# Transposes of softmax weights in longer runs on TensorE

## The chip, the cores and the metric

The kernel runs on one core of one Trainium2 chip. The metric is the device time of one execution in microseconds. The core's engines run side by side, each in the order of its own instruction stream, and wait for each other by semaphores: TensorE (PE; its weight loads are listed as PEld), VectorE (DVE), ScalarE (ACT), GpSimd (POOL) and SyncE (SP), which issues most of the transfers.

## The reference, cut to what matters

One encoder layer is applied to two sequences of 2048 tokens, each 1024 wide. Two attentions work side by side on one normed input, their outputs are gated and joined, and an output projection and a gated addition follow.

```python
proj = rms_norm(x, norm_w) @ w_in
q_a, k_a, v_a, g_a, q_b, k_b, v_b, g_b = jnp.split(proj, IN_SPLITS, axis=-1)
...
o_a = windowed_gqa_sink(q_a, k_a, v_a, sink_a) * jax.nn.silu(g_a)
...
o_b = neighbourhood_attn(q_b, k_b, v_b, rpb_b) * jax.nn.silu(g_b)
x = x + jnp.concatenate([o_a, o_b], axis=-1) @ w_out
gate = jax.nn.sigmoid(x @ w_ple_gate)
return x + (p @ w_ple) * gate
```

In the first attention (A, eight query heads on two key heads) a token sees the tokens at most 128 away, with a learned sink in the softmax. In the second (B, eight heads) the tokens form a grid of 32 rows by 64 columns, and each sees a window of 8 by 16 with a learned bias.

## The kernel before, in words

All is float32. Operands of products are split into a high and a low part; a projection takes three products for one. TensorE's work is a stream of projection products into which the attention's steps are put at chosen places.

The loop at line 1253 runs over 96 steps. Steps 0 to 31 are first attention, a block of 128 tokens each, in two halves (one for each key head): 64 units. Steps 32 to 95 are second attention, a tile of 8 by 16 tokens and four heads each: 64 units. While a unit's attention steps are issued, the stream issues the projections of a later block: each 512-wide product counts 215 and each 256-wide one 112 (lines 554, 602, 635, 883, 910). A step of first attention has 13008 of this count, its two halves half of it each; one of second attention has 10320, that is 48 products.

Where an attention step stands in the stream is written in three tables of (share of the unit, 1 for this unit or 0 for the one before, act, index): `PLAN_A` for first attention, `PLAN_C` for 51 units of second attention (`copied_`, line 112), and `PLAN_B` for its other 13. `plan` sorts the entries by share, and entries of one share keep their order. The loop lets the stream run until its count has reached an entry's share and then issues the act. TensorE's instructions keep this order exactly (`pinned`, line 272); those of the other engines are ordered by the framework's scheduler from their dependences and their place in the program, unless `P` pins them.

The acts that matter here:

- `sc`: scores of a head or pair into a PSUM tile, which VectorE adds to the mask or bias and writes to SBUF with the maximum (line 306).
- `exp`: exponentials on ScalarE (line 331). In the units of `PLAN_C`, a DMA from ScalarE's queue then copies each head's weights into a tile `tn` of another type (line 340); in first attention `turn` does it into `tna`, from SyncE's queue. Transposes of copied tiles are at line 291, of others at line 293.
- `pt`: transposes a group of the softmax weights on TensorE into a PSUM tile. In first attention there are three groups for a unit, of two, four and four transposes; in second attention one for each of the four heads, of three or four. ScalarE then copies the group as the high part (lines 813, 819, 1059) and VectorE subtracts for the low part (lines 814, 821, 1060).
- `po`: the product of transposed weights and values. `fin`: transposes the gate into PSUM, multiplies and stores.

PSUM tiles come from three sets (`PSB`, line 72). Scores, groups of transposed weights and the gate's transposes all take from the set `sc`, which has three buffers used in turn (`PSM`, line 73): a taker waits until the one three places before it has been read. For a unit of second attention the takers are four scores, the gate of the unit before and four groups, nine in all. The projections' results take from `pj`, the others from `ms`.

Of the kernel before, what the change touches and what calls it, by code (L numbers as in the profile page):

```python
# [58 lines left out]
def bias_offsets():  # L59
# [32 lines left out]
KB = 23  # L92
PLAN_A = (
    (0.04, 1, "sc", 0), (0.08, 1, "sc", 1), (0.11, 1, "sc", 2), (0.12, 1, "rest", 0), (0.14, 1, "sc", 3),
    (0.14, 1, "rest", 1), (0.21, 0, "pt", 0), (0.26, 0, "pt", 1), (0.30, 1, "qcopy", 0), (0.31, 0, "pt", 2),
    (0.32, 1, "exp", 0), (0.33, 1, "turn", 0), (0.33, 1, "turn", 1), (0.44, 1, "twice", 0),
    (0.48, 0, "po", 0), (0.56, 0, "po", 1), (0.64, 1, "prep", 0), (0.66, 0, "po", 2), (0.67, 1, "den", 0), (0.74, 0, "fin", 0),
    (0.75, 1, "gcopy", 0),
# [6 lines left out]
PLAN_C = (  # L105
    (0.00, 1, "sc", 0), (0.01, 0, "po", 0), (0.03, 1, "sc", 1), (0.05, 0, "po", 1), (0.07, 1, "sc", 2), (0.09, 0, "po", 2),
    (0.11, 1, "sc", 3), (0.16, 0, "po", 3), (0.16, 1, "exp", 0), (0.24, 0, "fin", 0), (0.35, 1, "prep", 0),
    (0.64, 1, "pt", 0), (0.73, 1, "pt", 1), (0.82, 1, "pt", 2), (0.91, 1, "pt", 3),
)


# [1500 lines left out]
```

## Time and profile before

| what | value |
|---|---|
| median of 3 runs | 2419.87 us (2417.95 to 2422.71) |
| profiled execution, its own time | 2419.81 us |
| span of the profile | 2417.8 us |
| TensorE busy | 2406.4 us (100%) |
| VectorE busy | 1733.2 us (72%) |
| ScalarE busy | 1425.4 us (59%) |
| GpSimd busy | 850.8 us (35%) |

The span runs from the first instruction to the last. A matmul is counted as busy until its modelled end, and matmuls overlap in TensorE's pipeline; so a stretch on TensorE is best read from one start to the next, not from the busy time of one instruction.

### The profile page before, as it was taken

The page shows a single profiled execution, that of the slowest core. Times are in us where ns is not written, and L with a number is a line of the kernel's source. Part 1 is how long each engine was busy: PE and PEld are TensorE (multiplying, and loading weights), DVE is VectorE, ACT ScalarE, POOL GpSimd, SP SyncE. Part 2 cuts the span into 40 slices and gives each one's busy share as a digit, 9 for nine tenths or more (in the row PEclk, how much of TensorE's full clock was granted, in tenths as well). Part 3 has the DMA queues.
Part 4 walks back from the last instruction along what each step waited for, and adds up shares of the span by engine and source line. Part 5 has one row for each costly group of instructions (what it writes and reads, how often), then busy time and mean ns, then how long its engine had stood idle before and what let it go on. Part 6 is the DMA issues. An engine that isn't in the chain of part 4 may idle for free.

```text
span 2417.8 us, 41537 instructions
## 1 busy us (share of the span) xinstructions
PE 2406.4 (100%) x12942; PEld 2031.4 (84%) x12942; DVE 1733.2 (72%) x4227; ACT 1425.4 (59%) x3408; POOL 850.8 (35%) x1373
## 2 busy tenths in 40 slices
PE   9999999999999999999999999999999999999999
PEld 7888888888888888888888888888888888888887
DVE  7888888888875776666667666776537565776876
ACT  6777777777764665666566666666753222344433
POOL 4555555556553554454445434443100000000000
PEclk9999999999999999999999999999999999999999
DMA  7665555655665677678877777778886455856765
GB/s 238 223 199 198 197 192 160 197 194 198 215 223 171 224 233 245 227 232 262 272 232 227 253 250 245 245 261 281 318 287 221 157 172 185 270 174 206 248 224 173
DMA packets 313660, 539.61 MB, mean 223 GB/s; under 512 B 36288, under 2 KB 136416, under 8 KB 309216
## 3 DMA queue, kind: packets, MB, share of 16 engines
q1 hardware_dynamic: 283776, 497.77, 61.6%
q10 hardware_dynamic: 29664, 39.19, 5.3%
q8 instruction: 104, 1.70, 0.3%
q14 instruction: 116, 0.95, 0.1%
HBM read 307.72 MB, written 134.23 MB: 183 GB/s over the span
## 4 chain that ended last, share of the span: by engine, by line
PE 95%; DMA 2%; ACT 1%; DVE 1%; issue 0%; POOL 0%; ACTq 0%; SPq 0%; DVEq 0%
PE pqk L287 14%; PE pvg L287 14%; PE acca L1402 14%; PE accc L1402 11%; PE pg L287 7%; PE pq L287 7%; PE pple L287 4%; PE scb L287 4%; PE pk L287 3%; PE pob L287 3%; PE po L287 3%; PE sc L287 3%; PE ptb L291 2%; PE pt L291 2%; PE ptb L293 1%; PE pktb L293 1%
## 5 line engine op out<-in xcount | busy, mean ns | idle before, releaser
L287 PE MATMUL pvg<-wb,xr 128*128 128x512 f32 x1536 | 472.4, 408 | 0.5 <-DMA wb<-sp_1wb 0.4
L287 PE MATMUL pqk<-wa,xr 128*128 128x512 f32 x1536 | 431.2, 408 | 0.0
L331 ACT ACTIVATE s<-s,nm 128x320 f32<-128x320 f32 (+6 forms) x512 | 294.5, 579 | 38.6 <-DVE nm L324 29.0
L287 PEld LDWEIGHTS pvg<-wb,xr 128*128 128x128 f32 x1536 | 272.8, 189 | 33.6 <-DMA wb<-sp_1wb 1.6
L287 PEld LDWEIGHTS pqk<-wa,xr 128*128 128x128 f32 x1536 | 264.9, 188 | 39.3
L1384 ACT CAST opd<-raw 128x512 fp32r<-128x512 f32 x224 | 131.5, 618 | 269.7 <-PE acca L1402 116.9
L417 POOL TENSOR_TENSOR xr<-stx,xr 128x512 fp32r<-128x512 f32 x186 | 238.0, 1296 | 102.0 <-ACT xr L416 71.6
L1385 DVE TENSOR_TENSOR opd<-raw,opd 128x512 fp32r<-128x512 f32 x224 | 146.3, 685 | 146.4 <-ACT opd L1384 146.4
L287 PE MATMUL pq<-wa,xr 128*128 128x512 f32 x768 | 240.5, 404 | 0.0
L287 PE MATMUL pg<-wb,xr 128*128 128x512 f32 x768 | 229.9, 405 | 0.7 <-DVE vv L574 0.4
L306 DVE CUSTOM_DVE_ANT_0 s<-scb,bias 128x288 f32<-128x288 f32 (+3 forms) x256 | 139.2, 547 | 71.2 <-PE scb L287 48.8
L1078 ACT COPY otb<-pob 64x512 f32<-64x512 f32 x128 | 74.3, 581 | 183.2 <-PE pob L287 182.6
L1402 PE MATMUL accc<-opd,wb 128*128 128x512 f32 x768 | 176.7, 389 | 0.0
L1402 PE MATMUL acca<-opd,wa 128*128 128x512 f32 (+1 forms) x780 | 175.9, 386 | 0.5 <-ACT raw L1487 0.5
L1402 PE MATMUL acca<-opd,s 128*128 128x512 f32 x768 | 175.4, 389 | 0.0
L1402 PEld LDWEIGHTS acca<-opd,wa 128*128 128x128 f32 x780 | 145.0, 188 | 30.2 <-ACT raw L1487 0.7
L1402 PEld LDWEIGHTS accc<-opd,wb 128*128 128x128 f32 x768 | 144.2, 188 | 29.9
L1402 PEld LDWEIGHTS acca<-opd,s 128*128 128x128 f32 x768 | 144.2, 188 | 29.9
L170 POOL TENSOR_TENSOR yb<-vrb,power 128x8 f32<-128x8 f32 x64 | 106.2, 1660 | 143.5 <-DVE vrb L898 130.9
L287 PEld LDWEIGHTS pg<-wb,xr 128*128 128x128 f32 x768 | 135.4, 188 | 17.8 <-DVE vv L574 0.8
L287 PEld LDWEIGHTS pq<-wa,xr 128*128 128x128 f32 x768 | 132.4, 188 | 11.4
L306 DVE CUSTOM_DVE_ANT_0 s<-sc,mask 128x320 f32<-128x320 f32 (+2 forms) x256 | 121.1, 478 | 19.2 <-PE sc L287 10.9
(209 smaller groups left out, 5122.4 us busy)
## 6 DMA issues: line engine op xcount, KB each, us to landing
tna<-s SPq DMA_DIRECT2D x112, 320.0 KB
stx<-x_b SPq DMA_DIRECT2D x128, 256.0 KB
vw<-v_d SPq DMA_DIRECT2D x96, 256.0 KB
v_d<-vb SPq DMA_DIRECT2D x64, 256.0 KB
xres<-x_r SPq DMA_DIRECT2D x64, 256.0 KB
raw<-x_d SPq DMA_DIRECT2D x16, 1024.0 KB
stx<-x_a SPq DMA_DIRECT2D x62, 256.0 KB
stn<-x_n SPq DMA_DIRECT2D x62, 256.0 KB
```

The costliest lines, as they stand in the source:

```text
L170: nc.gpsimd.tensor_tensor(out=y, in0=v, in1=power.broadcast_to([128, n]), op=ALU.pow)
L287: pinned(nc.tensor.matmul(out, lhsT, rhs, start=start, stop=stop))
L291: pinned(nc.tensor.transpose(out.bitcast(F32R), in_, eye))
L293: pinned(nc.tensor.transpose(out, in_, eye.bitcast(F32)))
L306: nc.vector.tensor_tensor_reduce(out=s, in0=ps[:, :n], in1=bias, scale=1.0, scalar=-3.0e38, op0=ALU.add, op1=ALU.max, accum_out=sm["mx"][: ...
L331: ex = nc.scalar.activation(ss[i], ss[i], AF.Exp, bias=nm[:, i:i + 1], accum_out=den[:, i:i + 1])
L417: low.tensor_tensor(out=lo, in0=raw, in1=hi.bitcast(F32), op=ALU.subtract)
L1078: nc.scalar.copy(ot[a:a + 64], pq[z:z + 64])
L1384: P(nc.scalar.copy(hi, v))
L1385: P(nc.vector.tensor_tensor(out=lo, in0=v, in1=hi.bitcast(F32), op=ALU.subtract))
L1402: pinned(nc.tensor.matmul(ps[:, cols], w[k][:, a, c:c + 128], o[:, b, cols], start=i in (0, 1, 4) and k == 0 and j == 0, stop=k == 3 and j ...
```

## The change

Six shares of two tables are altered; nothing else is. In first attention group 0 and group 1 get one share, so that their transposes (two and four) follow each other with no projection product between. In the 51 units of second attention that `PLAN_C` serves, the four heads' groups become two pairs, each of six to eight transposes in a row. `PLAN_B` is as before.

```diff
 PLAN_A = (
...
-    (0.14, 1, "rest", 1), (0.21, 0, "pt", 0), (0.26, 0, "pt", 1), (0.30, 1, "qcopy", 0), (0.31, 0, "pt", 2),
+    (0.14, 1, "rest", 1), (0.235, 0, "pt", 0), (0.235, 0, "pt", 1), (0.30, 1, "qcopy", 0), (0.31, 0, "pt", 2),
...
 PLAN_C = (
...
-    (0.64, 1, "pt", 0), (0.73, 1, "pt", 1), (0.82, 1, "pt", 2), (0.91, 1, "pt", 3),
+    (0.70, 1, "pt", 0), (0.70, 1, "pt", 1), (0.87, 1, "pt", 2), (0.87, 1, "pt", 3),
 )
```

## Rows read from the trace of the kernel before

**Rows 1.** The page's engine table: busy time, share of the span, instructions.

```profile
PE 2406.4 (100%) x12942; PEld 2031.4 (84%) x12942; DVE 1733.2 (72%) x4227; ACT 1425.4 (59%) x3408; POOL 850.8 (35%) x1373
```

**Rows 2.** The page's chain of waits, by engine, as shares of the span.

```profile
PE 95%; DMA 2%; ACT 1%; DVE 1%; issue 0%; POOL 0%; ACTq 0%; SPq 0%; DVEq 0%
```

**Rows 3.** Windows: stretch, length, busy time of each engine, clock, DMA.

```profile
50.00:700.00 650.00, 648.83 (x3991) 565.75 (x3990) 545.41 (x1628) 494.57 (x1352) 359.25 (x761) 1.00 0.61 202
772.00:1129.00 357.00, 356.67 (x1979) 299.35 (x1978) 245.15 (x613) 218.83 (x523) 179.24 (x209) 1.00 0.72 234
```

**Rows 4.** Timeline of TensorE in first attention: start, length, engine, line, what.

```profile
412.31 0.29 PE L291 MATMUL pt<-ident,tna 128*128 128x128 f32 x2
412.44 0.70 PE L287 MATMUL pg<-wb,xr 128*128 128x512 f32 x2
412.97 0.45 PE L291 MATMUL pt<-ident,tna 128*128 128x128 f32 x4
413.26 0.47 PE L287 MATMUL pg<-wb,xr 128*128 128x512 f32 x1
413.57 0.46 PE L291 MATMUL pt<-ident,tna 128*128 128x128 f32 x4
```

**Rows 5.** Timeline of TensorE in second attention, a unit and a later stretch.

```profile
999.51 0.37 PE L291 MATMUL ptb<-rowwise,tn 128*128 128x128 f32 x3
999.72 1.39 PE L287 MATMUL pqk<-wa,xr 128*128 128x512 f32 x5
...
1000.94 0.37 PE L291 MATMUL ptb<-rowwise,tn 128*128 128x128 f32 x3
1001.15 1.17 PE L287 MATMUL pqk<-wa,xr 128*128 128x512 f32 x4
...
1003.36 0.38 PE L291 MATMUL ptb<-rowwise,tn 128*128 128x128 f32 x3
...
1013.12 1.86 PE L287 MATMUL pqk<-wa,xr 128*128 128x512 f32 x7
1014.83 0.34 PE L291 MATMUL ptb<-rowwise,tn 128*96 128x128 f32 x3
```

**Rows 6.** The tiles of transposed weights: transposes of copied tiles, durations in ns.

```profile
L291 PE MATMUL pt<-ident,tna x560: 221/228/256, 71.3 to 706.3; 128*128 128x128 f32 x187
...
L291 PE MATMUL ptb<-rowwise,tn x660: 220/227/284, 776.2 to 1639.8; 128*128 128x128 f32 x90, 128*96 128x128 f32 x42, 128*120 128x128 f32 x33
```

**Rows 7.** Second attention's subtractions in all, and three units' timelines of three engines.

```profile
L1060 DVE TENSOR_TENSOR p_t<-ptb,p_t x192: 439/476/542, 778.3 to 1768.1; 120x288 fp32r<-120x288 f32 x48, 128x368 fp32r<-128x368 f32 x48, 96x320 fp32r<-96x320 f32 x24, 128x320 fp32r<-128x320 f32 x24
...
824.23 0.41 ACT L1059 CAST p_t<-ptb 96x320 fp32r<-96x320 f32 x1
...
824.96 0.48 DVE L1060 TENSOR_TENSOR p_t<-ptb,p_t 96x320 fp32r<-96x320 f32 x1
...
826.65 0.34 PE L291 MATMUL ptb<-rowwise,tn 128*96 128x128 f32 x3
...
999.92 0.41 ACT L1059 CAST p_t<-ptb 128x304 fp32r<-128x304 f32 x1 [0.96 <-PE ptb L291]
...
1002.37 0.85 DVE L1060 TENSOR_TENSOR p_t<-ptb,p_t 128x304 fp32r<-128x304 f32 x2
...
1513.24 0.85 DVE L1060 TENSOR_TENSOR p_t<-ptb,p_t 128x304 fp32r<-128x304 f32 x2
...
1513.78 0.44 PE L291 MATMUL ptb<-rowwise,tn 128*128 128x128 f32 x3
```

**Rows 8.** Timeline of TensorE where a group waited for a transfer.

```profile
923.80 0.50 PE L291 MATMUL ptb<-rowwise,tn 128*128 128x128 f32 x4 [0.33 <-DMA tn<-s]
...
1402.02 0.41 PE L291 MATMUL ptb<-rowwise,tn 128*120 128x128 f32 x3 [0.43 <-DMA tn<-s]
```

**Rows 9.** Timelines of VectorE and TensorE around a product of the weights.

```profile
427.18 0.68 DVE L814 TENSOR_TENSOR pr<-pt,pr 128x512 fp32r<-128x512 f32 x1
...
427.90 0.63 PE L287 MATMUL po<-pr,vv 128*128 128x512 f32 x2
```

## The prediction

> **What bounds the kernel now.** I read the page's engine table first: TensorE is busy for 2406.4 of the 2417.8 us span, the next engine (VectorE) for 72% [rows 1]. A busy share alone can hide waiting, so the chain of waits came next: 95% of it is TensorE's own instructions, 2% DMA, 1% each ScalarE and VectorE [rows 2]. Then the two stretches that the edits touch: in first attention TensorE is never free and VectorE runs 545 of 650 us; in second attention VectorE runs 245 of 357 us; the granted clock is 1.00 in both, the upper of its two levels (2.4 GHz) [rows 3]. So every nanosecond that TensorE issues less is gained, and every nanosecond that it waits is lost. There is no cover for either. The instruction order on TensorE is the written one, so only two questions remain: what a longer run of transposes saves, and what the new places make TensorE wait for.
>
> **Where the groups move.** The emission counts 215 for each 512-wide projection product and starts an act when the count reaches its share. In second attention's copied units (total 10320) the shares 0.64, 0.73, 0.82, 0.91 are reached after 31, 36, 40 and 44 products: gaps of five, four, four, and the rows show just these (five products from 999.72, four from 1001.15) [rows 5]. After the edit 0.70 is reached after 34 products and 0.87 after 42. So group 0 starts three products later, group 1 two earlier, group 2 two later, group 3 two earlier, and between the pairs lie eight products. In first attention (13008 for two halves) 0.21 and 0.26 stand one product apart in the first half and two in the second; 0.235 puts group 0 one product later in both, and group 1 one earlier in the second half.
>
> **What one merge is worth.** The first product behind a run of transposes takes 0.31 us from its start to the next start: 413.26 to 413.57 [rows 4]; I take 0.30, since the rows are rounded. A stretch of seven takes 1.71 us (1013.12 to 1014.83) with such a first one, so the others take (1.71 - 0.30)/6 = 0.235 [rows 5]. Each run that disappears saves 0.30 - 0.235 = 0.065, or 0.07 us. Against this, transposes get slower in a longer run. A run of two takes 0.13 us until the next product starts (412.31 to 412.44), one of four 0.29 (412.97 to 413.26), so the third and fourth cost 0.08 each [rows 4]; a run of three takes 0.21 [rows 5]. Runs of six do not occur in these stretches; I extend the 0.08 to 0.085 of the last two, which makes 0.29 + 0.165 = 0.455. First attention: 0.13 + 0.29 + 0.07 = 0.49 becomes 0.455, a gain of 0.035. Second attention: 0.21 + 0.21 + 0.07 = 0.49 becomes 0.455 as well. These rows are rounded to 0.01, so I allow 0.02 to 0.035 a merge and take 0.025.
>
> The trace shows the shape of a rule in the Trainium skill ("TensorE: Matmul & The Clock Gate", section Back-to-back issue gap): pairs of weight load and 128-wide matmul sustain about 81 ns each. The rows agree for the third and fourth transpose (0.08). If all six went at that pace, a run of six would take 0.486 us, the same as the two runs with their extra start; by the page alone the change would save nothing.
>
> **How many merges.** First attention has 560 transposes from the copied tiles, ten a unit (two, four, four): 56 units, one merge each. Second attention has 660 from copied tiles [rows 6] in the 51 units that the third plan serves, two merges each: 102. Together 158 merges at 0.025: 3.95 us (3.2 to 5.5 at the bounds). The eight units at the ends of the sequences, which transpose uncopied tiles, I leave at zero; 0.03 each either way is 0.2 us.
>
> **What the new places wait for: the buffer of group 3.** Scores, gate transposes and weight transposes share three PSUM buffers in turn. With nine takers a unit, group 3 takes the buffer of group 0, which is free once ScalarE's copy (line 1059) and VectorE's subtraction (line 1060) of group 0 are done. Group 3 stood 3.85 us behind group 0's old place (999.51 to 1003.36). In the new order it starts 0.70 (three products) + 0.455 + 0.30 + 7 x 0.235 + 0.21 = 3.3 us behind that old place: 0.55 us earlier, while group 0 itself comes 0.70 later. I set the two against each other in all 51 units, of which three kinds are shown [rows 7]:
> - At 824.96 the subtraction ends at 825.44; group 3 was at 826.65 and would be at 826.1. Room is 0.65 us, and ScalarE came to its copy at 824.23, over a microsecond behind the transposes (826.65 - 3.8 = 822.9, plus 0.2), so group 0's delay is mostly absorbed. 29 units have room of this sort even with all of group 0's delay added.
> - At 1002.37 the first of two subtractions ends at 1002.84; group 3 was at 1003.36 and would be at 1002.8. It is just too late already. Here the copy started as soon as the transposes ended (999.92, after 0.96 us of waiting for them), so if the order of ScalarE's work stays, the 0.70 us pass on in full and TensorE stands for 0.75 us, and with it the projection products queued behind group 3.
> - At 1513.24 the subtraction ends at 1513.72 and group 3 starts right behind it, at 1513.78: there the earlier place gains nothing and 0.55 us become a wait. Three units are like this.
> Added over 51 units: 2.1 us if the copy and the subtraction keep their present times, 9.2 us if each is late by the part of 0.70 us that ScalarE's idle time doesn't absorb (22 units wait). The lower value needs ScalarE's other copies to move ahead of group 0's. These are not pinned, their inputs are ready, and in the first kind of unit they already stand ahead; so I take 2.1 for the likeliest and keep 9.2.
>
> **What the new places wait for: the copies by DMA.** Each group reads a tile that a DMA has rewritten. Twice the fourth group waits for that landing: 0.33 us idle at 923.80 and 0.43 at 1402.02 [rows 8]. 0.55 us earlier it waits 0.55 longer. No view gives the landings of the others. The bound below is zero (the landings shift with other transfers), above I put five units at 0.55, 2.75; I take these two and part of a third: 1.4 us. Group 0 comes later and has no such wait.
>
> **First attention.** Group 0's own products are due (0.48 - 0.235) x 6504/215, some seven projection products, later, so its delay by one has room. But VectorE works without a gap there: the last subtraction (427.18, ends 427.86) finishes 0.04 us before the product that reads it starts (427.90) [rows 9]. A TensorE that is 0.025 us earlier can find it unready, so of 56 x 0.025 = 1.4 us I may lose the half, 0.7; it is inside the rounding of one merge, and I leave it in the range.
>
> **Sum.** The profiled execution took 2419.81 us (span 2417.8), the median of the runs is 2419.87; they agree to 0.06. 2419.81 - 3.95 + 2.1 + 1.4 = 2419.4 us.
>
> **Rivals.**
> 1. Clean gain: no new wait, 2419.81 - 3.95 = 2415.9. For it: the room in 29 units. Against: the three units without any, and the two DMA waits.
> 2. Slower, by one mechanism: group 3 waits for group 0's buffer because ScalarE keeps its order and so comes late to group 0's copy. 2419.81 - 3.95 + 9.2 + 1.4 = 2426.5. It decides from about 9 us of waiting, a mean of 0.18 us a unit. For it: at 999.92 ScalarE stood idle until group 0's transposes ended, so a later group 0 is passed on to all that follows there [rows 7]. Against: other copies could go first.
> 3. All transposes of a run at the pace of 0.08 us: six take 0.48 to 0.49, the merges save nothing, the waits remain: 2419.81 + 3.5 = 2423.3. The page named above would have it so. Against: a run of two takes 0.13, not 0.16.
> 4. A larger saving: 0.035 a merge (5.5 us) and no new wait, 2414.3. For it: the rounded rows allow it.
>
> **How the numbers follow.** Changes within 0.2% (4.8 us) can't be told from none here. Chances: the forecast 0.39, rival 1 0.20, rival 2 0.25, rival 3 0.05, rival 4 0.11, which gives faster 0.12, same 0.62 and slower 0.26 (a little of the forecast's own upper end lies over the limit). The forecast's own range is 2416 to 2424; with rival 1 whole and most of rivals 2 and 4 it becomes 2414.6 to 2427.
>
> **What would show it.** TensorE's timeline: runs of six with starts 0.45 to 0.46 us before the next product, eight products between pairs, and only the first of these at 0.30. Right behind group 2 in second attention, idle time ended by line 1060 or by the landing of a copy: under 4 us in all for the forecast, near 10 for rival 2. A run of six at 0.49 would be rival 3. I am wrong altogether if ScalarE's and VectorE's orders in first attention change so that the products of the weights wait there; the unit shown has 0.04 us of room, and 64 units would multiply what goes over it.

## The result, and the profile after

The changed kernel takes 2430.89 us (median of 5 runs, 2429.38 to 2432.11), the kernel before 2419.87 (5 runs on the same chip): a ratio of 1.0043, 95% interval 1.0028 to 1.0058. It is slower by 11 us, outside the stated range (2414.6 to 2427), and the forecast was no change that can be told. The profiled execution took 2431.21 us, its span is 2429.4.

The page after, the engine table and the chain of waits by engine:

```profile
PE 2409.6 (99%) x12942; PEld 2035.6 (84%) x12942; DVE 1731.7 (71%) x4227; ACT 1419.8 (58%) x3408; POOL 851.4 (35%) x1373
...
PE 90%; DVE 3%; ACT 3%; DMA 2%; issue 1%; ACTq 1%; POOL 0%; SPq 0%; DVEq 0%
```

TensorE has the same 12942 matmuls and 3.2 us more of busy time [rows 1], while the span grew by 11.6; what grew is mostly the time in which it waits. In the chain its share fell from 95% [rows 2] to 90%, and VectorE and ScalarE rose from one each to three each. So something on those two engines now ends last, again and again.

Where that is shows in the first and last start of two sorts of matmul. Second attention's first projection product (`pqk`) stands near the end of first attention's stretch; its scores (`scb`) run through second attention. The tile views of the two kernels, before and then after (first and last start are the two times behind the durations):

```profile
L287 PE MATMUL pqk<-wa,xr x1536: 387/396/481, 674.9 to 1666.0; 128*128 128x512 f32 x192
...
L287 PE MATMUL scb<-ks_b,q1b x256: 290/338/401, 767.6 to 1761.5; 128*128 128x288 f32 x32, 128*128 128x384 f32 x32, 128*128 128x360 f32 x32, 128*128 128x480 f32 x32
```

```profile
L287 PE MATMUL pqk<-wa,xr x1536: 387/393/481, 684.3 to 1676.8; 128*128 128x512 f32 x192
...
L287 PE MATMUL scb<-ks_b,q1b x256: 290/338/389, 777.0 to 1772.2; 128*128 128x288 f32 x32, 128*128 128x384 f32 x32, 128*128 128x360 f32 x32, 128*128 128x480 f32 x32
```

At the first `pqk` the changed kernel is 9.4 us behind (684.3 against 674.9), at the first scores still 9.4, at the last scores 10.7. First attention, where the forecast expected a gain of 1.4 us, holds nearly all of the loss.

The products that read group 0 are the two of `po<-pr` and `po<-pr,twice`, called the edge products from here on. One first half of a step, on TensorE, ScalarE and VectorE of the changed kernel:

```profile
450.83 0.62 PE L291 MATMUL pt<-ident,tna 128*128 128x128 f32 x6
451.29 0.69 PE L287 MATMUL pq<-wa,xr 128*128 128x512 f32 x2
451.82 0.46 PE L291 MATMUL pt<-ident,tna 128*128 128x128 f32 x4
452.11 1.38 PE L287 MATMUL pq<-wa,xr 128*128 128x512 f32 x5
453.33 0.31 PE L287 MATMUL po<-pr 128*128 128x256 f32 x1
453.80 0.36 PE L287 MATMUL po<-pr,twice 128*128 128x256 f32 x1 [0.17 <-DVE pr L821]
454.00 0.62 PE L287 MATMUL pq<-wa,xr 128*128 128x512 f32 x2
...
451.31 0.56 ACT L331 ACTIVATE s<-s,nm 128x320 f32<-128x320 f32 x1 [1.69 <-DVE nm L327]
...
451.99 0.76 ACT L819 CAST pr<-pt 64x256 fp32r<-64x256 f32 x2
...
452.78 0.88 DVE L821 TENSOR_TENSOR pr<-pt,pr 64x256 fp32r<-64x256 f32 x2 [0.47 <-ACT pr L819]
```

The same place in the kernel before:

```profile
444.79 0.29 PE L291 MATMUL pt<-ident,tna 128*128 128x128 f32 x2
...
447.56 0.28 PE L287 MATMUL po<-pr 128*128 128x256 f32 x1
447.67 0.28 PE L287 MATMUL po<-pr,twice 128*128 128x256 f32 x1
447.79 0.40 PE L287 MATMUL pq<-wa,xr 128*128 128x512 f32 x1
...
445.17 0.76 ACT L819 CAST pr<-pt 64x256 fp32r<-64x256 f32 x2 [1.36 <-PE pt L291]
445.95 0.56 ACT L331 ACTIVATE s<-s,nm 128x320 f32<-128x320 f32 x1
...
446.39 0.88 DVE L821 TENSOR_TENSOR pr<-pt,pr 64x256 fp32r<-64x256 f32 x2
```

The reader should look at lines 819 and 331 on ScalarE. Before, the two copies of group 0 come first and an exponential follows. From the start of group 0's transposes to the copies it takes 0.38 us (444.79 to 445.17). After, an exponential comes first (451.31), and the copies start at 451.99, 1.16 us after the run of six began (450.83). VectorE, which needs each copy for its subtraction (line 821), stands idle for 0.47 us, its two subtractions end near 453.66, and the second edge product starts at 453.80 instead of right behind the first. Before, the subtractions ended near 447.27, 0.40 us ahead of the second edge product (447.67). From the first edge product to the next projection product it takes 454.00 - 453.33 = 0.67 us instead of 447.79 - 447.56 = 0.23: 0.44 us lost.

The waits that TensorE's matmuls had in the changed kernel (what waited, releaser, us in total, times, longest):

```profile
PE po L287 <- DVE pr L821: 4.2, 24, 0.4
PE ptb L291 <- DMA tn<-s: 2.9, 3, 1.2
PE ptb L291 <- DVE p_t L1060: 2.7, 6, 1.3
```

The first line is that wait, 24 times. One of the 24, the longest (0.4 us), has a like in the kernel before; the other 23 have 3.8 us. This understates them, since a matmul counts as busy to its modelled end and that hides the first part of each wait. The starts show more. Summed over the two traces, the time from the first edge product to the next product behind the edge products is 28.3 us after and 17.2 before: 11.1 us more, of which 10.4 stand in 23 first halves that lose 0.41 to 0.48 each. Less the 1.8 us that the merges measured by themselves (merged at the old place, below), this leaves 9.3, and 9.4 were found. The other two lines are second attention's waits at group 3, which the forecast had expected: for a copy's landing and for the buffer of group 0.

### The profile page after: what moved, and what is told of

The parts are those of the page before. It is cut to its first block, busy times and chain, and to the rows that moved or that the text cites. A ratio compares the mean times of both kernels' runs of the same rounds, so it can differ in the third digit from the quotient of the medians.

```text
span 2429.4 us, 41556 instructions
## 1 busy us (share of the span) xinstructions
PE 2409.6 (99%) x12942; PEld 2035.6 (84%) x12942; DVE 1731.7 (71%) x4227; ACT 1419.8 (58%) x3408; POOL 851.4 (35%) x1373
## 4 chain that ended last, share of the span: by engine, by line
PE 90%; DVE 3%; ACT 3%; DMA 2%; issue 1%; ACTq 1%; POOL 0%; SPq 0%; DVEq 0%
PE acca L1402 14%; PE pvg L287 13%; PE pqk L287 13%; PE accc L1402 11%; PE pg L287 7%; PE pq L287 5%; PE scb L287 4%; PE pk L287 3%; PE pob L287 3%; PE pple L287 3%; PE po L287 3%; PE sc L287 3%; PE ptb L291 2%; PE pt L291 1%; DMA tn<-s 1%
## 5 line engine op out<-in xcount | busy, mean ns | idle before, releaser
L287 PE MATMUL pqk<-wa,xr 128*128 128x512 f32 x1536 | 405.7, 402 | 0.0
L287 PEld LDWEIGHTS pqk<-wa,xr 128*128 128x128 f32 x1536 | 272.9, 188 | 47.4
L287 PE MATMUL pq<-wa,xr 128*128 128x512 f32 x768 | 234.3, 401 | 0.0
L287 PE MATMUL pg<-wb,xr 128*128 128x512 f32 x768 | 224.1, 403 | 0.4 <-DVE vv L574 0.4
L306 DVE CUSTOM_DVE_ANT_0 s<-sc,mask 128x320 f32<-128x320 f32 (+2 forms) x256 | 121.5, 478 | 19.9 <-PE sc L287 11.6
```

Source lines behind the costliest of these rows:

```text
L287: pinned(nc.tensor.matmul(out, lhsT, rhs, start=start, stop=stop))
L306: nc.vector.tensor_tensor_reduce(out=s, in0=ps[:, :n], in1=bias, scale=1.0, scalar=-3.0e38, op0=ALU.add, op1=ALU.max, accum_out=sm["mx"][: ...
```

## The experiments

All ratios are of a kernel to the kernel before on the same chip, with the 95% interval. Medians of the kernel before in the three sets were 2420.16, 2421.31 and 2419.76 us.

**First attention's edit alone.**

```diff
-    (0.21, 0, "pt", 0), (0.26, 0, "pt", 1)
+    (0.235, 0, "pt", 0), (0.235, 0, "pt", 1)
```

> Only the first attention's two shares are changed; second attention is as before. Theory 1 (the loss sits in first attention, where in the first half of each step an exponential now goes ahead of group 0's two copies on ScalarE and the edge product waits): the whole of first attention's 9.4 us stays, about +9.4 us on the kernel before, with idle time of 0.3 to 0.4 us at the edge product in some 25 first halves. Theory 2 (group 3's buffer and the copies by DMA in second attention make the loss): no loss here, -1.4 us from 56 merges.

Measured: 2429.45 us, ratio 1.0034 (1.0022 to 1.0047). The loss is there without the other edit; theory 2 falls.

**Second attention's edit alone.**

```diff
-    (0.64, 1, "pt", 0), (0.73, 1, "pt", 1), (0.82, 1, "pt", 2), (0.91, 1, "pt", 3)
+    (0.70, 1, "pt", 0), (0.70, 1, "pt", 1), (0.87, 1, "pt", 2), (0.87, 1, "pt", 3)
```

> Only second attention's four shares are changed. Theory 1: its merges save 2.5 us, its waits for group 0's buffer and for copies cost 3 to 6 us; +1 to +3 us on the kernel before, first attention as before. Theory 2: +9 us or more.

Measured: 2422.12 us, ratio 1.0006 (0.9997 to 1.0014). As theory 1 has it; the interval includes no change.

**An order edge for one exponential.** `last_cp` holds the second copy of line 819, and `behind` puts an instruction after another of the same engine.

```diff
-    (0.21, 0, "pt", 0), (0.26, 0, "pt", 1)
+    (0.235, 0, "pt", 0), (0.235, 0, "pt", 1)
...
             ex = nc.scalar.activation(ss[i], ss[i], AF.Exp, bias=nm[:, i:i + 1], accum_out=den[:, i:i + 1])
+            if sink is not None and n_ == 0 and last_cp:
+                behind(ex, last_cp[-1])
```

> First attention's merge at 0.235 as in the change, second attention as before, and one order edge more: the first exponential of a unit stands behind the second copy of group 0 on ScalarE. Theory 1 (the order on ScalarE makes the loss): the idle time at the edge product goes, -1.4 us on the kernel before (0 to -2). Theory 3 (group 0's later place itself is too late for its product, whatever the order): the loss stays, near +9 us.

Measured: 2430.86 us, ratio 1.0043 (1.0031 to 1.0056). The loss stays, but the edit had not done what it was to do. ScalarE and TensorE in this kernel (old line numbers from 334 on are two higher, those behind the copies of old line 819 four higher):

```profile
170.75 0.56 ACT L331 ACTIVATE s<-s,nm 128x320 f32<-128x320 f32 x1 [1.70 <-DVE nm L327]
...
171.43 0.76 ACT L821 CAST pr<-pt 64x256 fp32r<-64x256 f32 x2
...
173.24 0.36 PE L287 MATMUL po<-pr,twice 128*128 128x256 f32 x1 [0.16 <-DVE pr L825]
```

An exponential still precedes the copies: a unit has four, they are not pinned among each other, and another one had taken the place. So this run tells nothing between theories 1 and 3.

**The order edge for all four.**

```diff
-            if sink is not None and n_ == 0 and last_cp:
+            if sink is not None and last_cp:
                 behind(ex, last_cp[-1])
```

> As a_exp_behind_copies, but all four exponentials of a unit stand behind the second copy of group 0, not the first alone: there another of the four had gone ahead (the timeline shows an exponential at 170.75 and the copies at 171.43). Theory 1 (the order on ScalarE): the idle time at the edge product of the first halves goes; -1.4 us on the kernel before (0 to -2). Theory 3 (group 0's later place itself): near +9 us.

Measured: 2420.24 us, ratio 0.9996 (0.9987 to 1.0005). With group 0 in the change's place and the runs merged, the loss is gone:

```profile
445.30 0.63 PE L291 MATMUL pt<-ident,tna 128*128 128x128 f32 x6
...
445.68 0.76 ACT L821 CAST pr<-pt 64x256 fp32r<-64x256 f32 x2 [1.59 <-PE pt L291]
446.46 0.59 ACT L815 CAST pr<-pt 128x512 fp32r<-128x512 f32 x1
446.94 0.57 ACT L331 ACTIVATE s<-s,nm 128x320 f32<-128x320 f32 x1
...
447.81 0.28 PE L287 MATMUL po<-pr 128*128 128x256 f32 x1
447.93 0.28 PE L287 MATMUL po<-pr,twice 128*128 128x256 f32 x1
448.05 0.40 PE L287 MATMUL pq<-wa,xr 128*128 128x512 f32 x1
```

The copies come first, 0.38 us after the run of six began, and from the first edge product to the next projection it takes 0.24 us again. Theory 3, that the later place is by itself too late for its product, falls.

**Group 0 late, nothing merged.**

```diff
-    (0.21, 0, "pt", 0), (0.26, 0, "pt", 1)
+    (0.235, 0, "pt", 0), (0.28, 0, "pt", 1)
```

> First attention alone: group 0 at 0.235 as in the change, but group 1 at 0.28, so that no run is merged. Theory 1: an exponential goes ahead of the late group 0's copies as in the change, the loss stays without the merges' gain: +9 to +11 us on the kernel before. Theory 4 (the merging makes the loss): no change, within 1 us.

Measured: 2428.98 us, ratio 1.0034 (1.0021 to 1.0046), some 8 us; the lower end of what was expected, 9 us, lies in the interval.

```profile
170.23 0.56 ACT L331 ACTIVATE s<-s,nm 128x320 f32<-128x320 f32 x1 [1.71 <-DVE nm L327]
...
170.91 0.76 ACT L819 CAST pr<-pt 64x256 fp32r<-64x256 f32 x2
```

No run is longer than before, and the exponential is ahead all the same. The place of group 0 changes the order, not the merging, and theory 4 falls. (Group 1 stands a little later here as well, 0.28 instead of 0.26; in first attention's edit alone it doesn't, and the loss is the same.)

**Merged at the old place.**

```diff
-    (0.21, 0, "pt", 0), (0.26, 0, "pt", 1)
+    (0.21, 0, "pt", 0), (0.21, 0, "pt", 1)
```

> Groups 0 and 1 of first attention merged at the old place of group 0 (0.21), second attention as before. Theory 1: group 0 is not later, its copies stay ahead of the exponentials, no new idle time: -1.4 us (0 to -2). Theory 4 (the longer run itself makes the loss, wherever it stands, by bringing group 1 and its copy closer): near +9 us as with the change.

Measured: 2418.32 us, ratio 0.9989 (0.9980 to 0.9998).

```profile
168.05 0.62 PE L291 MATMUL pt<-ident,tna 128*128 128x128 f32 x6
168.51 0.92 PE L287 MATMUL pq<-wa,xr 128*128 128x512 f32 x3
...
168.43 0.76 ACT L819 CAST pr<-pt 64x256 fp32r<-64x256 f32 x2 [1.36 <-PE pt L291]
```

The same run of six, with the copies ahead, is a small gain.

Counted over whole traces, an exponential stands directly ahead of group 0's copies in 28 of first attention's 64 units, all of them first halves, in each of the four kernels of first attention's loss (the change, its first attention alone, the edge for one exponential, group 0 late and unmerged). It does so in 2 units of the kernel before and of this one, and in none with the edge for all four.

**Second attention's pairs at the outer places.**

```diff
-    (0.70, 1, "pt", 0), (0.70, 1, "pt", 1), (0.87, 1, "pt", 2), (0.87, 1, "pt", 3)
+    (0.64, 1, "pt", 0), (0.64, 1, "pt", 1), (0.91, 1, "pt", 2), (0.91, 1, "pt", 3)
```

> Second attention alone: both pairs at the outer places (0.64 twice, 0.91 twice), so that group 0 and group 3 stand where they stood and no group 3 comes early. Both the theory of group 0's buffer and that of the DMA copies expect the waits at group 3 to go: the merges' 2.5 us remain, -2.5 us on the kernel before (-1.5 to -3). If the longer runs were worth nothing: 0.

Measured: 2416.38 us, ratio 0.9978 (0.9969 to 0.9987), more than expected: 3 to 7.5 us.

**Only the second pair as early as in the change.**

```diff
-    (0.70, 1, "pt", 0), (0.70, 1, "pt", 1), (0.87, 1, "pt", 2), (0.87, 1, "pt", 3)
+    (0.64, 1, "pt", 0), (0.64, 1, "pt", 1), (0.87, 1, "pt", 2), (0.87, 1, "pt", 3)
```

> Second attention alone: the first pair at 0.64, the second at 0.87 as in the change. Group 3 is as early as in the change, but group 0 has its old place. Theory B (group 3 waits for group 0's buffer): most of the waits go, -1.5 to -2.5 us on the kernel before. Theory D (group 3 waits for the landing of its copy): the waits of the change stay, about +1.5 to +2 us.

Measured: 2420.74 us, ratio 0.9996 (0.9988 to 1.0005), between the two theories. The waits of TensorE at the groups tell them apart, in second attention's edit alone and then in this kernel:

```profile
PE ptb L291 <- DVE p_t L1060: 3.5, 7, 0.9
...
PE ptb L291 <- DMA tn<-s: 1.5, 2, 0.9
```

```profile
PE ptb L291 <- DMA tn<-s: 1.4, 4, 0.5
...
PE ptb L291 <- DVE p_t L1060: 0.4, 1, 0.4
```

Group 0 in its old place takes the wait for its buffer from 3.5 to 0.4 us and leaves the wait for the copies at 1.4. Not all of that is group 3's: two of its four waits, 0.69 us, are those of group 1, the second of the first pair, which now stands where group 0 stands:

```profile
839.53 0.44 PE L291 MATMUL ptb<-rowwise,tn 128*120 128x128 f32 x3 [0.20 <-DMA tn<-s]
...
1240.36 0.46 PE L291 MATMUL ptb<-rowwise,tn 128*128 128x128 f32 x3 [0.49 <-DMA tn<-s]
```

Each list is of one execution, and second attention's places of the change gave 2.7 (buffer) and 2.9 us (copies) in the whole change, but 3.5 and 1.5 in the edit alone. So group 0's late place as the cause of most of the buffer waits is clear of that spread; that a group moved earlier waits for its copy's landing is seen at groups 1 and 3, but its cost is not settled.

**The change with the order edge.** The diff is the whole change and that of the edge for all four.

> The whole change, with all four exponentials of a unit of first attention behind the second copy of group 0. Theory 1: first attention's loss goes, what is left is second attention's +2 us: +0.5 to +2.5 us on the kernel before, 8 to 10 us below the change. If the two parts of the change hinder each other: over +4 us.

Measured: 2419.65 us, ratio 0.9997 (0.9988 to 1.0006). The edge takes the loss away: the kernel is 0.1 us below the kernel before, where +0.5 to +2.5 us were expected (0.5 lies in the interval), and 11.2 us below the change, where 8 to 10 were.

**Both merges at the better places.** First attention 0.21 twice; second attention 0.64 twice and 0.91 twice.

> First attention's groups 0 and 1 merged at 0.21, second attention's pairs at 0.64 and 0.91. The two parts were measured alone at -1.8 and -4.9 us. If they add, -6 to -7 us on the kernel before, about 2413.5; if one part's gain was chance or both draw on the same slack, -3 to -5.

Measured: 2414.47 us, ratio 0.9976 (0.9966 to 0.9986): faster than both kernels, by 5.3 us than before. That is less than the sum of the two alone (6.8 us by medians); the intervals don't settle whether anything is shared.

## Why the prediction was wrong, point by point

- **Places and runs: right.** The runs of six stand as worked out (450.83 to 451.29, 0.46 us, against 0.455), eight products lie between second attention's pairs, and two behind the run of six take 0.53 us (451.29 to 451.82), one of them at the longer start. Six 128-wide transposes of second attention take the same:

```profile
996.15 0.63 PE L291 MATMUL ptb<-rowwise,tn 128*128 128x128 f32 x6
996.62 2.08 PE L287 MATMUL pqk<-wa,xr 128*128 128x512 f32 x8
998.54 0.63 PE L291 MATMUL ptb<-rowwise,tn 128*128 128x128 f32 x6
999.00 1.16 PE L287 MATMUL pqk<-wa,xr 128*128 128x512 f32 x4
```

- **The worth of a merge: right in kind, too small in second attention.** 56 merges without new waits gave 1.8 us by medians (forecast 1.4), 102 at the outer places gave 4.9 (forecast 2.55). Waits don't explain the second number: the list of TensorE's waits at second attention's groups has 0.8 us in the kernel before and 0.6 at the outer places. Summed from one start to the next over these two traces, projection products (`pqk`) take 10.4 us less and the transposes 5.3 more. A merge takes away one first product of 0.30 us, as forecast, but deep in the longer stretch a product takes 0.228 us, not 0.235; and two runs of three 96-wide transposes (0.18 us each) become one of 0.39, where the forecast priced every pair by the 128-wide rows.
- **Rival 3 (all transposes at one pace, no gain) falls**, since merges gained wherever they brought no new wait, and since a run of six 128-wide transposes takes 0.46 to 0.47 us. The Trainium skill ("TensorE: Matmul & The Clock Gate", section Back-to-back issue gap) gives about 81 ns for each pair of weight load and 128-wide matmul; six of them would be 0.486 us, an estimate that these rows stay below.
- **Second attention's waits: right in kind, too small in size.** Group 3 waits for group 0's buffer and for copies, as rows 7 and 8 had foretold. In the unit of 1513.78 [rows 7] the changed kernel shows it: the run is torn between groups 2 and 3, while the first of two subtractions ends near 1524.2.

```profile
1523.59 0.38 PE L291 MATMUL ptb<-rowwise,tn 128*128 128x128 f32 x3
1524.29 0.45 PE L291 MATMUL ptb<-rowwise,tn 128*128 128x128 f32 x3 [0.33 <-DVE p_t L1060]
...
1523.76 0.85 DVE L1060 TENSOR_TENSOR p_t<-ptb,p_t 128x304 fp32r<-128x304 f32 x2
```

  The forecast's sign was under 4 us of such listed waits; the change has 5.6 and second attention's edit alone 5.0, so that sign failed. The edit alone (+2.0 us) and the one at the outer places (-4.9) merge the same runs and differ by 6.9 us by medians, against 3.5 us of waits in the sum. Net, the forecast's terms for second attention come to -2.55 + 2.1 + 1.4 = +1.0 us, and alone it measured +2: that this is close is luck, since both the merges and the waits came out at about twice their terms by medians, and the two misses cancel.
- **First attention: wrong, and this is the step that failed.** The prediction said that group 0's own products are due some seven projection products later, "so its delay by one has room", gave this no term in the sum, and kept 0.7 us in the range for another subtraction, the unit's last [rows 9]. The room was counted from TensorE's places alone; without saying so, it took ScalarE to do the same things in the same order, a product later. But group 0's copies are not pinned, and with the group one product later the scheduler's order came out with an exponential ahead of them. They then stand behind an exponential and its accumulator, 0.68 us (451.31 to 451.99), and the room at the second edge product had been 0.40 us. In place of a gain of 1.4 us first attention lost 9.4. The runs with and without the order edge show it, with the same places on TensorE: 2429.45 us without (ratio 1.0034), 2430.86 with an edge that left the order as it was (1.0043), 2420.24 with the edge that turned it round (0.9996). Why the scheduler turns the order when the group moves by one product is not shown.
- **The rivals.** Rival 2 had the right kind of mechanism (ScalarE comes late to group 0's copy) in the wrong attention, and with the opposite condition: it needed ScalarE to keep its order. In second attention it had 22 units wait for group 0's buffer; the change lists six such waits. The last sentence of the prediction named a change of order in first attention as what would make it altogether wrong, but gave it no price and no chance. The price could have been estimated: one exponential with its accumulator (0.68 us) less the room at the edge product (0.40), in 28 first halves, is about 8 us. Rivals 1 and 4 had no new wait, and the waits above rule both out for these places; at the better places, where the waits for copies and buffers at the groups were no larger than before, 2414.47 us is near what rival 4 had (2414.3).

## What to carry to other kernels

When a step is moved by even one product, ask of every engine that serves it in which order its work will now be issued, and price the case that a longer instruction gets ahead of the short one that the bottleneck waits for. An instruction whose result the bottleneck needs soon (here with 0.40 us to spare) should be held in its place by an order edge, against all of its competitors and not the first alone. Merging short runs on TensorE is worth 0.03 to 0.05 us a merge here, so it pays only where both partners keep the dates of their buffers and copies. The version at 0.21, 0.64 and 0.91 leaves group 0 of both attentions and group 3 where they stood, and moves their partners to them.

## What the runs showed that I had not expected

In 23 first halves of first attention's steps the edge products lost 0.41 to 0.48 us each, while all second halves together lost 0.7 us, with the same edit. And the waits listed for them (3.8 us) show less than half of what the starts show (10.4 us), because a waiting matmul's idle time is counted only from the modelled end of the one before it.
